# Where the running sums of a conditioning vector lie, and which engine adds to them

## The chip, the cores and the metric

The kernel runs on one core of one Trainium2 chip. The metric is the device time of one execution in microseconds (us), smaller is better. Three runs of the kernel before gave 2071.96, 2072.45 and 2074.96 us, so the median is 2072.45 us. A further execution was taken with the hardware profiler, and all rows of the profile come from that one.

## What is computed

One decoder layer, 1024 positions of width 2048, all in fp32. Cut to what matters here:

```python
mod = silu(c) @ W_ada + b_ada            # (1, 6144): shift | scale | gate, 2048 each
h   = rms_norm(x) * (1 + scale) + shift  # (1024, 2048)
proj = h @ W_in                          # (1024, 8192): q,k,v,z of 8 + 8 heads
...                                      # stick-breaking attention, retention, gating
out = x + gate * (concat(oa, ob) @ W_out)
```

`mod` is a product of one row of 2048 numbers with a matrix of 2048 x 6144, so W_ada is 48 MB that is read once and used for one multiply-add for each number. This is the *conditioning*. `h`'s first 1024 columns need only the first half of shift and scale. So the kernel computes the first half of the conditioning at its start, begins with the first half of the depth of `h @ W_in`, and does the conditioning's second half (the rest of shift and scale, and the gate) beside those matmuls. The change is in that second half.

## The kernel before, in words

**The large products.** Each of the three fp32 products is cut into groups of 256 output columns and half of the depth. A group is done with seven products instead of eight (a Strassen-Winograd scheme: `P1` to `P7`, line 32), each of depth 512 in four steps. An fp32 operand is split in a high and a low part, and a step is three matmuls 128x128 by 128x512 (`mm3`, lines 149 to 152), so a product is 12 matmuls. There are 16 groups in the first stage (`groups_a`); its tiles are named with an `e` in the profile: `b_e`, `a_e`, `d_e` are PSUM banks that take products, `wr_e` the raw weights, `wh_e_P` and `wl_e_P` their high and low parts. For every product ScalarE (ACT) makes the high part (line 259) and VectorE (DVE) the low part (line 264: raw minus high, both from SBUF); GpSimd (POOL) makes sums and differences of weight blocks (line 254); DVE also adds finished banks onto tiles in SBUF (line 293, one operand in PSUM) and ACT copies banks out (line 284). The third matmul of a step in the program's order uses `wl_e_P` (line 152 in the profile).

**The order of the work.** Each engine works through a list in order, and these lists are written out by the program itself, not by a scheduler: one *tick* is one step of a product (three matmuls). `at(k, fn)` records `fn`'s instructions k ticks later; generators such as `second_half` are continued when the number of ticks that they yielded has passed. So the place of every instruction in its engine's queue is fixed by ticks, and at run time an engine that waits holds up all that stands behind it. All the large loads and stores are issued from one queue (SyncE, SP), also in order.

**The second half of the conditioning** (`second_half`, lines 592 to 653). Line 408 views W_ada so that partition p holds rows 16p to 16p+15. For each of eight column blocks i of 512 columns, 16 tiles 128x512 (r = 0 to 15) are loaded into a ring of four buffers (`sg`, shown as `ada_b`), three rows ahead; the load of row n+3 takes the buffer of row n-1. Rows come every 2 or 3 ticks. Row r of block i is handled so:

- For i below 4 (shift and scale) DVE does all 16 rows with `weigh`: the first is a multiplication by the column `silu_c[:, r]` (line 433), the other 15 are `acc = row * column + acc` in one instruction (SCALAR_TENSOR_TENSOR, line 435). The running sum `acc_b` lies in SBUF.
- For i from 4 on (the gate) DVE does the even rows alone. Odd rows are multiplied by ACT (line 631 for r = 1, line 633 in place for the others) and added to a second running sum by POOL (line 635, two ticks later). The buffer of such a row is free when POOL has added it.

Ten ticks after a block's last row, `close` sums over the partitions (`over_partitions`, lines 410 to 414): the running sum is the matmuls' weight operand, four 128x128 pieces, and a column of ones is the moving operand. With two running sums there are eight such matmuls. The profile shows two records for each, so 8 records in a close for i below 4 and 16 for i from 4 on. The result is one column of a PSUM bank (`mod_b`, bank C), from which DVE takes it three ticks later (lines 419 to 421, or 617).

`keep_left` (lines 655 to 664) runs beside it: POOL adds high and low parts into `kp` tiles (line 661) and SP stores them. PSUM has eight banks: four for the products (`pj0` to `pj3`), and `A0`, `A1`, `B`, `C`. In the stretch of `second_half` the program uses of the latter four only `C`.

Of the kernel before, what the change touches and what calls it, by code (L numbers as in the profile page):

```python
# [11 lines left out]
F32 = mybir.dt.float32  # L12
F32R = mybir.dt.float32r
I32 = mybir.dt.int32
AF = mybir.ActivationFunctionType
ALU = mybir.AluOpType

P = 128
# [8 lines left out]
HALF = 512  # L27
# [32 lines left out]
def layer_kernel(ctx, tc, x, c, w_ada, b_ada, norm_gain, w_in, sb_q_gain, sb_k_gain, ret_norm_gain, w_out,  # L60
                 rot, ret_mask, ret_kdec, chunk_decay, out):
    nc = tc.nc
# [7 lines left out]
    ps = ctx.enter_context(tc.tile_pool(name="ps", bufs=1, space=PS))  # L70
# [36 lines left out]
    silu_c = cons.tile([P, 16], F32, name="silu_c")  # L107
# [57 lines left out]
    def at(k, fn):  # L165
        later.append((now[0] + k, fn))
# [243 lines left out]
    def over_partitions(mod, accs_):  # L410
        for i in range(4):
            for acc in accs_:
                nc.tensor.matmul(mod[:, i:i + 1], acc[:, i * P:(i + 1) * P], ones, start=acc is accs_[0],
                                 stop=acc is accs_[-1])

    def ada_mod(j, mod):

        k2 = slice(2 * j, 2 * j + 2)
        nc.vector.tensor_tensor(a_c[:, k2], mod[:, 2:4], scale_b1[:, k2], op=ALU.add)
        nc.vector.tensor_tensor(a_c[:, k2], a_c[:, k2], gain_c[:, k2], op=ALU.mult)  # L420
        nc.vector.tensor_tensor(s_c[:, k2], mod[:, 0:2], shift_b[:, k2], op=ALU.add)
# [4 lines left out]
    def to_h(t, kc):  # L426
        nc.scalar.activation(t, t, AF.Identity, scale=a_c[:, kc:kc + 1], bias=s_c[:, kc:kc + 1])

    def weigh(acc, src, r, first):

        cj = silu_c[:, r:r + 1]
        if first:
            nc.vector.tensor_scalar(acc, src, cj, None, op0=ALU.mult)
        else:
            nc.vector.scalar_tensor_tensor(acc, src, cj, acc, op0=ALU.mult, op1=ALU.add)  # L435
# [153 lines left out]
    k1b = Ring(k1p2.__enter__())  # L589
    ctx.enter_context(tc.manual_schedule(engines=set(ENGINES)))  # L590

    def second_half():

        order_ = [(i, r) for i in range(8) for r in range(16)]
        src, accs_ = {}, {}

        def load(n):
            if n < len(order_):
                i, r = order_[n]
                src[i, r] = t = k1b.tile([P, HALF], F32, tag="sg", bufs=4, name=f"ada_b{i}_{r}")  # L600
                if i < 4:
                    j = NP + i
                    nc.sync.dma_start(t.rearrange("p (a n) -> p a n", a=2),
                                      ada_rows[:, r, 0:2, 256 * j:256 * j + 256])
                else:
                    nc.sync.dma_start(t, ada_rows[:, r, 2, HALF * (i - 4):HALF * (i - 3)])

        def close(i):
            mod = ps.tile([P, 4], F32, tag="C", name=f"mod_b{i}")
            over_partitions(mod, accs_.pop(i))  # L610

            def take_mod():
                if i < 4:
                    ada_mod(NP + i, mod)
                else:
                    k4 = slice(4 * (i - 4), 4 * (i - 3))
                    nc.vector.tensor_tensor(gate_c[:, k4], mod, gate_b[:, k4], op=ALU.add)
            at(3, take_mod)

        for n in range(3):  # L620
            load(n)
        yield 9
        for n, (i, r) in enumerate(order_):
            if r == 0:
                accs_[i] = [k1b.tile([P, HALF], F32, tag="acc", bufs=2, name=f"acc_b{i}")]
            t = src.pop((i, r))
            if i < 4 or r % 2 == 0:
                weigh(accs_[i][0], t, r, r == 0)
            elif r == 1:
                accs_[i].append(k1b.tile([P, HALF], F32, tag="acc2", bufs=2, name=f"acc2_b{i}"))  # L630
                nc.scalar.activation(accs_[i][1], t, AF.Copy, scale=silu_c[:, r:r + 1])
            else:
                nc.scalar.activation(t, t, AF.Copy, scale=silu_c[:, r:r + 1])
                a2 = accs_[i][1]
                at(2, lambda a2=a2, t=t: nc.gpsimd.tensor_tensor(a2, a2, t, op=ALU.add))
            if r == 15:
                at(10, lambda i=i: close(i))
            load(n + 3)
            yield 2 + n % 2
        yield 16  # L640
        for j in range(NP):
            kc = KC // 2 + 2 * j
            a11, a12, a21, a22 = xT[kc, 0], xT[kc + 1, 0], xT[kc, 1], xT[kc + 1, 1]
            for t, k in ((a11, kc), (a21, kc), (a22, kc + 1), (a12, kc + 1)):
                to_h(t, k)
                yield 2
            s1 = k1b.tile([P, HALF], F32, tag="sg", bufs=4, name=f"S1_{j}")
            nc.gpsimd.tensor_tensor(s1, a21, a22, op=ALU.add)
            yield 2
            nc.gpsimd.tensor_tensor(a21, a11, a21, op=ALU.subtract)  # L650
            yield 2
            staged.update({("A11", j): a11, ("S3", j): a21, ("S1", j): s1, ("A12", j): a12, ("A22", j): a22})
        ready.add("h2")

    def keep_left():
# [8 lines left out]
        ready.add("keep")  # L664

    start(second_half(), 4)
    start(keep_left(), 40, 0)

# [693 lines left out]
```

## Time and profile before

| what | value |
|---|---|
| median of three runs | 2072.45 us |
| the profiled execution's own time | 2072.09 us |
| its span from first to last instruction | 2070.3 us |
| mean granted TensorE clock | 0.98 |
| PE busy | 1957.0 us, 95% of the span |
| DVE, ACT, POOL busy | 1427.0, 941.0, 925.6 us |
| first and last multiply-add of the second half | 132.6 and 377.8 us after the span's start |

Between the span and the execution's own time lie 1.8 us that no instruction shows. The conditioning's second half takes the stretch from about 130 to 385 us, about an eighth of the span.

How rows are read: a group of instructions is given as line, engine, operation, output <- inputs, shapes, count, then busy time in us and mean ns of one, and behind the second bar the idle time of the engine just before them and what ended it. In rows of three durations these are the shortest, the median and the longest, in ns. A row of waits gives the waiting engine with its tile and line, what it waited for, us in total, how often, and the longest. A row of a window gives from and to, its length, and for each engine busy us and the number of instructions, then the granted clock (`PEclk`), the busy share of the DMA engines, and GB/s.

### The profile page before, as it was taken

To read this page: it belongs to the slowest core of one execution; us is meant where nothing else is said; L and a number is where in the kernel's file an instruction comes from. 1 tells how busy PE (TensorE), PEld (TensorE's weight loads), DVE (VectorE), ACT (ScalarE), POOL (GpSimd) and SP (SyncE) were. 2 spreads that over 40 slices of the span, in tenths; PEclk is the share of its full clock that TensorE was granted. 3 is DMA by queue.
4 is the path that set the end of the run, shared out by engine and by line. 5 is a ranking of instruction groups with operands and counts; after the bars stand their busy time and mean duration, and the time that the engine had idled before them with its cause. 6 is when DMAs were issued, how large, how long until landed. Compare 5 with 4: busy or idle time off the path is not lost. (4 is left out here: it accounts for less than half of the span.)

```text
span 2070.3 us, 27207 instructions
## 1 busy us (share of the span) xinstructions
PE 1957.0 (95%) x9089; PEld 1564.0 (76%) x9089; DVE 1427.0 (69%) x2098; ACT 941.0 (45%) x1718; POOL 925.6 (45%) x627
## 2 busy tenths in 40 slices
PE   5879999998999999999999999899999998998998
PEld 4458777775768677788888888687788876886887
DVE  6779877566668675776766655788687887448555
ACT  4443344554455545554444444544353545345222
POOL 0434577765444235232322312677465654145443
PEclk9879999999999999999999999999999999999999
DMA  8748877533454444443433523867576877457665
GB/s 295 234 126 275 269 235 255 163 107 117 151 171 153 138 143 163 146 160 115 158 121 112 177 93 128 273 214 260 190 257 214 275 257 238 145 170 236 199 197 175
DMA packets 287329, 388.45 MB, mean 188 GB/s; under 512 B 32106, under 2 KB 164276, under 8 KB 287188
## 3 DMA queue, kind: packets, MB, share of 16 engines
q1 hardware_dynamic: 286784, 386.65, 56.9%
q8 instruction: 72, 1.18, 0.2%
q14 instruction: 69, 0.57, 0.1%
q10 hardware_dynamic: 404, 0.05, 0.0%
HBM read 278.51 MB, written 108.10 MB: 187 GB/s over the span
## 5 line engine op out<-in xcount | busy, mean ns | idle before, releaser
L264 DVE TENSOR_TENSOR wl_e_P<-wr_e,wh_e_P 128x512 fp32r<-128x512 f32 x560 | 528.9, 945 | 218.1 <-ACT wh_e_P L259 213.1
L254 POOL TENSOR_TENSOR wr_e<-wr_e,wr_e 128x512 f32<-128x512 f32 x240 | 354.6, 1492 | 495.3 <-DVE wl_e_P L264 445.7
L259 ACT ACTIVATE wh_e_P<-wr_e 128x512 fp32r<-128x512 f32 x560 | 350.7, 628 | 276.1 <-PE b_o L151 28.1
L254 POOL TENSOR_TENSOR wr_e<-wr_e 128x512 f32<-128x512 f32 x80 | 112.9, 1411 | 134.5 <-DVE wl_e_P L264 120.3
L915 DVE TENSOR_TENSOR_SCAN om<-om 128x128 f32<-128x128 f32 (+2 forms) x96 | 120.1, 1251 | 56.7 <-ACT om L906 54.9
L287 POOL TENSOR_TENSOR u_e<-u_e,c_e 128x512 f32<-128x512 f32 x50 | 79.0, 1583 | 114.9 <-DMA c_e<-part 71.8
L287 POOL TENSOR_TENSOR p_e<-p_e,c_e 128x512 f32<-128x512 f32 x49 | 74.9, 1529 | 102.2 <-DMA c_e<-part 59.4
L435 DVE SCALAR_TENSOR_TENSOR acc_b<-ada_b,silu_c,acc_b 128x512 f32<-128x512 f32 x88 | 97.3, 1106 | 27.4 <-DMA ada_b<-in_w_ada_dram 26.9
L152 PE MATMUL b_e<-S_h,wl_e_P 128*128 128x512 f32 x192 | 77.6, 404 | 7.9 <-DVE wl_e_P L264 7.7
L150 PE MATMUL b_e<-S_h,wh_e_P 128*128 128x512 f32 x192 | 77.1, 401 | 5.7 <-ACT p_e L284 5.7
L921 DVE TENSOR_TENSOR be<-be,om 128x127 f32<-128x127 f32 (+2 forms) x96 | 76.0, 792 | 7.8
L152 PE MATMUL b_h<-S_h,wl_e_P 128*128 128x512 f32 x192 | 75.7, 394 | 4.2 <-DVE wl_e_P L264 4.2
L151 PE MATMUL b_h<-S_l,wh_e_P 128*128 128x512 f32 x192 | 75.3, 392 | 3.4 <-DVE S_l L147 2.4
L962 PE MATMUL oT<-a,v 128*128 128x256 f32 x320 | 76.8, 379 | 0.0
L150 PE MATMUL b_h<-S_h,wh_e_P 128*128 128x512 f32 x192 | 76.7, 400 | 0.0
L151 PE MATMUL b_e<-S_l,wh_e_P 128*128 128x512 f32 x192 | 76.5, 398 | 0.0
L150 PE MATMUL b_f<-S_h,wh_e_P 128*128 128x512 f32 x192 | 76.3, 398 | 0.0
L150 PE MATMUL b_g<-S_h,wh_e_P 128*128 128x512 f32 x192 | 75.8, 395 | 0.0
L152 PE MATMUL b_f<-S_h,wl_e_P 128*128 128x512 f32 x192 | 74.9, 390 | 0.4 <-DVE wl_e_P L264 0.4
L151 PE MATMUL b_f<-S_l,wh_e_P 128*128 128x512 f32 x192 | 74.9, 390 | 0.0
L152 PE MATMUL b_g<-S_h,wl_e_P 128*128 128x512 f32 x192 | 74.9, 390 | 0.0
L151 PE MATMUL b_g<-S_l,wh_e_P 128*128 128x512 f32 x192 | 74.9, 390 | 0.0
(487 smaller groups left out, 5505.8 us busy)
## 6 DMA issues: line engine op xcount, KB each, us to landing
wr_e<-in_w_in_dram SPq DMA_DIRECT2D x128, 512.0 KB, 5.5
ada_b<-in_w_ada_dram SPq DMA_DIRECT2D x128, 256.0 KB, 4.7
c_e<-part SPq DMA_DIRECT2D x128, 256.0 KB, 5.2
ada_a<-in_w_ada_dram SPq DMA_DIRECT2D x64, 256.0 KB, 4.4
wr_e<-in_w_out_dram SPq DMA_DIRECT2D x32, 512.0 KB, 4.8
ld<-fin SPq DMA_DIRECT2D x54, 256.0 KB, 4.7
part<-p_e SPq DMA_DIRECT2D x48, 256.0 KB, 5.3
part<-u_e SPq DMA_DIRECT2D x48, 256.0 KB, 2.1
```

The lines of the kernel that those rows point to most:

```text
L150: nc.tensor.matmul(o, a_hi, b_hi, start=first, stop=False, skip_group_check=True)
L151: nc.tensor.matmul(o, a_hi, b_lo, start=False, stop=False, skip_group_check=True)
L152: nc.tensor.matmul(o, a_lo, b_hi, start=False, stop=last, skip_group_check=True)
L254: nc.gpsimd.tensor_tensor(t[o], t[a], t[b], op=op)
L259: nc.scalar.activation(hi, self.t[RIGHT[p]], AF.Copy)
L264: nc.vector.tensor_tensor(lo, self.t[RIGHT[p]], self.parts[p].bitcast(F32), op=ALU.subtract)
L287: at(6, lambda: nc.gpsimd.tensor_tensor(t, t, o, op=ALU.add))
L435: nc.vector.scalar_tensor_tensor(acc, src, cj, acc, op0=ALU.mult, op1=ALU.add)
L915: nc.vector.tensor_tensor_scan(rev, rev, rev, init, op0=ALU.mult, op1=ALU.bypass)
L921: nc.vector.tensor_tensor(be[:, :m], be[:, :m], om[:, 1:m + 1], op=ALU.mult)
L962: nc.tensor.matmul(ob, v[:, j, :], a[:, cl], start=diag and ib == 0 and b == 0 and j2 == 0, stop=ch == 0 and ib == 2, skip_group_check=True)
```

## The change

The running sum `acc` of each of the eight blocks becomes a PSUM tile of 128x512, one whole bank, `A0` for even i and `A1` for odd i. DVE does all 16 rows of every block, for the gate too; ACT's multiplications and POOL's additions of odd rows (lines 631, 633, 635) and the second running sum are gone. Two ticks after a block's last row ACT copies the bank once into an SBUF tile `total` (`acc_s`), and `close`, at the same tick as before, sums that one tile over the partitions. Loads, their order, their buffers and the ticks are as they were.

```diff
             if r == 0:
-                accs_[i] = [k1b.tile([P, HALF], F32, tag="acc", bufs=2, name=f"acc_b{i}")]
-            t = src.pop((i, r))
-            if i < 4 or r % 2 == 0:
-                weigh(accs_[i][0], t, r, r == 0)
-            elif r == 1:
-                accs_[i].append(k1b.tile([P, HALF], F32, tag="acc2", bufs=2, name=f"acc2_b{i}"))
-                nc.scalar.activation(accs_[i][1], t, AF.Copy, scale=silu_c[:, r:r + 1])
-            else:
-                nc.scalar.activation(t, t, AF.Copy, scale=silu_c[:, r:r + 1])
-                a2 = accs_[i][1]
-                at(2, lambda a2=a2, t=t: nc.gpsimd.tensor_tensor(a2, a2, t, op=ALU.add))
+                acc = ps.tile([P, HALF], F32, tag=f"A{i % 2}", name=f"acc_b{i}")
+            weigh(acc, src.pop((i, r)), r, r == 0)
             if r == 15:
-                at(10, lambda i=i: close(i))
+                total = k1b.tile([P, HALF], F32, tag="acc", bufs=2, name=f"acc_s{i}")
+                at(2, lambda total=total, acc=acc: nc.scalar.activation(total, acc, AF.Copy))
+                at(10, lambda i=i, total=total: close(i, total))
```

`close` then calls `over_partitions(mod, [acc])` with that one tile.

How the queues change, first on DVE at the start of block i = 6 (`gate_c` closes block 5; `wl_e_P` is the low part of a weight, `u_e` and `p_e` take a finished bank). Before:

```order
L433 TENSOR_SCALAR acc_b_1317<-ada_b_0_1270,silu_c 128x512
L264 TENSOR_TENSOR wl_e_P_1263<-wr_e_0_1192,wh_e_P_1255 128x512
L435 SCALAR_TENSOR_TENSOR acc_b_1317<-ada_b_2_1274,silu_c,acc_b_1317 128x512
L264 TENSOR_TENSOR wl_e_P_1194<-wr_e_1_1199,wh_e_P_1190 128x512
L264 TENSOR_TENSOR wl_e_P_1201<-wr_e_0_1192,wh_e_P_1197 128x512
L617 TENSOR_TENSOR gate_c<-mod_b_2659,cols 128x4
```

The same place on DVE now:

```order
L433 TENSOR_SCALAR acc_b_2617<-ada_b_0_1270,silu_c 128x512
L264 TENSOR_TENSOR wl_e_P_1263<-wr_e_0_1192,wh_e_P_1255 128x512
L435 SCALAR_TENSOR_TENSOR acc_b_2617<-ada_b_1_1272,silu_c,acc_b_2617 128x512
L435 SCALAR_TENSOR_TENSOR acc_b_2617<-ada_b_2_1274,silu_c,acc_b_2617 128x512
L264 TENSOR_TENSOR wl_e_P_1194<-wr_e_1_1199,wh_e_P_1190 128x512
L435 SCALAR_TENSOR_TENSOR acc_b_2617<-ada_b_3_1319,silu_c,acc_b_2617 128x512
L264 TENSOR_TENSOR wl_e_P_1201<-wr_e_0_1192,wh_e_P_1197 128x512
L617 TENSOR_TENSOR gate_c<-mod_b_2652,cols 128x4
```

Each odd row of a gate block now stands on DVE between the low parts, 32 such instructions in all, as it did before for blocks 0 to 3.

On ACT, at the end of block 5 (`acc_s` is `total`, `wh_e_P` the high part of a weight, `p_e` and `c_e` copies of finished banks), now:

```order
L284 ACTIVATE p_e_1373<-b_e_2570 128x512
L259 ACTIVATE wh_e_P_1197<-wr_e_0_1192 128x512
L629 ACTIVATE acc_s_1730<-acc_b_2400 128x512
L259 ACTIVATE wh_e_P_1255<-wr_e_0_1192 128x512
L284 ACTIVATE c_e_1715<-b_e_2419 128x512
```

The copy out of PSUM (line 629 of the changed kernel) is new; it stands ahead of the next high part, and it must wait for DVE's last row of that block.

On PE, the close of block 5, before (the two tiles are DVE's and POOL's running sums):

```order
L152 MATMUL b_e_2577<-S_3_h,wl_e_P_1201 128x512
L413 MATMUL mod_b_2659<-ones,acc_b_1525 128x1
L413 MATMUL mod_b_2659<-ones,acc_b_2408 128x1
L413 MATMUL mod_b_2659<-ones,acc_b_1525 128x1
L413 MATMUL mod_b_2659<-ones,acc_b_2408 128x1
L413 MATMUL mod_b_2659<-ones,acc_b_1525 128x1
L413 MATMUL mod_b_2659<-ones,acc_b_2408 128x1
L413 MATMUL mod_b_2659<-ones,acc_b_1525 128x1
L413 MATMUL mod_b_2659<-ones,acc_b_2408 128x1
L150 MATMUL d_e_2672<-S_0_h,wh_e_P_1255 128x512
```

and now:

```order
L151 MATMUL b_e_2570<-S_3_l,wh_e_P_1197 128x512
L152 MATMUL b_e_2570<-S_3_h,wl_e_P_1201 128x512
L413 MATMUL mod_b_2652<-ones,acc_s_1730 128x1 x4
L150 MATMUL d_e_2661<-S_0_h,wh_e_P_1255 128x512
L151 MATMUL d_e_2661<-S_0_l,wh_e_P_1255 128x512
```

Four of the eight matmuls of each gate block's close are gone; for blocks 0 to 3 the count stays at four.

More of the change, by code (lines that the diff above doesn't have):

```diff
@@ L594, in second_half @@
         order_ = [(i, r) for i in range(8) for r in range(16)]
-        src, accs_ = {}, {}
+        src = {}
         def load(n):
@@ L606, in load, with close @@
                     nc.sync.dma_start(t, ada_rows[:, r, 2, HALF * (i - 4):HALF * (i - 3)])
-        def close(i):
+        def close(i, acc):
             mod = ps.tile([P, 4], F32, tag="C", name=f"mod_b{i}")
-            over_partitions(mod, accs_.pop(i))
+            over_partitions(mod, [acc])
             def take_mod():
```

## The prediction, made before the changed kernel ran

> **What bounds the kernel now.** The page first, for who is busy; then the groups of DVE in the stretch of the second half; then windows between the closes, for where PE loses time; then waits and single durations, for why.
>
> ```profile
> PE 1957.0 (95%) x9089; PEld 1564.0 (76%) x9089; DVE 1427.0 (69%) x2098; ACT 941.0 (45%) x1718; POOL 925.6 (45%) x627
> core 0: us, PE busy (x) PEld busy (x) DVE busy (x) ACT busy (x) POOL busy (x), PEclk, DMA share, GB/s
> 163.00:193.00 30.00, 29.90 (x139) 24.54 (x139) 26.50 (x32) 10.47 (x18) 15.15 (x11) 1.00 0.89 289
> 193.00:223.00 30.00, 28.05 (x119) 21.73 (x118) 27.29 (x35) 8.22 (x14) 13.77 (x9) 1.00 0.72 236
> 223.00:255.00 32.00, 29.33 (x131) 23.41 (x131) 25.81 (x33) 8.62 (x15) 15.08 (x10) 1.00 0.85 276
> 286.00:317.00 31.00, 29.71 (x132) 23.46 (x132) 23.04 (x22) 13.42 (x23) 24.69 (x16) 1.00 0.73 243
> 317.00:351.00 34.00, 31.95 (x130) 24.57 (x130) 25.63 (x23) 14.60 (x26) 25.21 (x18) 0.90 0.83 282
> ```
>
> PE is the bound: the time is PE's work plus the gaps in it. In this stretch DVE is busy for 74 to 91% of a window, and PE has gaps.
>
> How much is lost shows between the closes. From the timeline of PE, the closes of blocks 0, 4 and 7:
>
> ```profile
> 161.68 0.39 PE L152 MATMUL b_e<-S_h,wl_e_P 128*128 128x512 f32 x1
> 163.04 0.39 PE L152 MATMUL b_e<-S_h,wl_e_P 128*128 128x512 f32 x1
> 163.27 0.95 PE L413 MATMUL mod_b<-ones,acc_b 128*128 128x1 f32 x8
> 164.40 0.39 PE L151 MATMUL b_e<-S_l,wh_e_P 128*128 128x512 f32 x1
> ...
> 284.97 0.39 PE L152 MATMUL b_e<-A_h,wl_e_P 128*128 128x512 f32 x1
> 285.20 1.92 PE L413 MATMUL mod_b<-ones,acc_b 128*128 128x1 f32 x16
> 287.29 0.40 PE L151 MATMUL d_e<-A_l,wh_e_P 128*128 128x512 f32 x1
> ...
> 383.16 2.15 PE L413 MATMUL mod_b<-ones,acc_b 128*128 128x1 f32 x16
> ```
>
> Six matmuls from 161.68 to 163.04 give a pitch of 0.227 us, so a product of 12 takes 2.72. A close of 8 records puts 164.40 - 163.04 = 1.36 where two pitches (0.45) would stand: it costs 0.91. One of 16 costs 2.32 - 0.45 = 1.87. Between two closes lie 40 ticks, 120 matmuls, 27.2 us. From 163.27 to 383.16 are 219.9 us; seven times 27.2 is 190.4, and the seven closes in it (four short, three long) 9.25. So 20.2 us are lost, 2.9 for each block. Who is waited for:
>
> ```profile
> PE b_e L152 <- DVE wl_e_P L264: 3.1, 6, 0.8
> PE d_e L152 <- DVE wl_e_P L264: 1.9, 2, 1.3
> ...
> SPq L606 <- POOL acc_b L635: 51.8, 19, 6.0
> SPq L606 <- DVE acc_b L435: 12.3, 12, 3.1
> ...
> 319.40 0.49 DVE L433 TENSOR_SCALAR acc_b<-ada_b,silu_c 128x512 f32<-128x512 f32 x1 [4.47 <-DMA ada_b<-in_w_ada_dram]
> ...
> 319.00:320.00 1.00, 0.89 (x2) 0.16 (x2) 0.60 (x2) 0.00 (x0) 0.00 (x0) 0.51 1.06 394
> 325.00:326.00 1.00, 1.00 (x4) 0.81 (x3) 0.24 (x1) 0.87 (x3) 1.00 (x2) 0.58 1.05 391
> ```
>
> These waits are of 252 to 390 us. PE waits for the low parts, thus for DVE. SP's queue stood 51.8 us waiting for POOL to free row buffers, loads came late, and DVE waited for rows with low parts queued behind (4.47 us before 319.40, for the first row of block 6). There PE's granted clock fell to a half from 319 to 325.6: 3.3 of the 20.2 us are clock, 16.9 waits.
>
> **The change part by part.** Why DVE is late, for 125 to 252 us (blocks 0 to 3), then for 252 to 390:
>
> ```profile
> L435 DVE SCALAR_TENSOR_TENSOR acc_b<-ada_b,silu_c,acc_b 128x512 f32<-128x512 f32 x60 | 61.1, 1019 | 11.4 <-DMA ada_b<-in_w_ada_dram 10.8
> L264 DVE TENSOR_TENSOR wl_e_P<-wr_e,wh_e_P 128x512 fp32r<-128x512 f32 x41 | 36.2, 883 | 8.1 <-ACT wh_e_P L259 8.1
> ...
> L264 DVE TENSOR_TENSOR wl_e_P<-wr_e,wh_e_P 128x512 fp32r<-128x512 f32 x44 | 58.7, 1335 | 10.8 <-ACT wh_e_P L259 10.8
> L435 DVE SCALAR_TENSOR_TENSOR acc_b<-ada_b,silu_c,acc_b 128x512 f32<-128x512 f32 x28 | 36.2, 1293 | 16.1 <-DMA ada_b<-in_w_ada_dram 16.0
> L433 DVE TENSOR_SCALAR acc_b<-ada_b,silu_c 128x512 f32<-128x512 f32 x4 | 3.4, 856 | 5.4 <-DMA ada_b<-in_w_ada_dram 5.4
> L635 POOL TENSOR_TENSOR acc_b<-acc_b,ada_b 128x512 f32<-128x512 f32 x28 | 43.8, 1564 | 15.6 <-ACT ada_b L633 15.1
> ```
>
> And single durations (shortest, median, longest), of instructions with two inputs in SBUF and with one in PSUM:
>
> ```profile
> L435 DVE SCALAR_TENSOR_TENSOR acc_b<-ada_b,silu_c,acc_b x88: 735/753/1787, 132.6 to 377.8; 128x512 f32<-128x512 f32 x88
> L264 DVE TENSOR_TENSOR wl_e_P<-wr_e,wh_e_P x560: 617/691/1819, 95.6 to 2055.4; 128x512 fp32r<-128x512 f32 x187
> L293 DVE TENSOR_TENSOR c_e<-b_h,c_e x16: 673/682/692, 1341.6 to 1715.1; 128x512 f32<-128x512 f32 x16
> L295 DVE SCALAR_TENSOR_TENSOR cp_o<-b_o,gate_c,cp_o x7: 749/751/752, 1940.0 to 2062.8; 128x512 f32<-128x512 f32 x7
> L284 ACT ACTIVATE c_e<-b_e x16: 577/598/600, 144.4 to 469.4; 128x512 f32<-128x512 f32 x16
> ```
>
> Where both inputs lie in SBUF, DVE takes 0.69 to 0.75 us or up to 1.82; with one in PSUM never over 0.752. Low parts take 883 ns on average beside a POOL without running sums and 1335 beside one with them. I read the long ones as DVE and POOL shutting each other out of SBUF.
>
> *Multiply-adds.* The 88 become 120. With the sum in PSUM the nearest row is L295's 0.75, the same operation with one input in PSUM; but it writes SBUF, and no row has DVE write PSUM. Bounds: 0.735, the shortest in SBUF, and two passes, 1.47. I take 0.75. First rows (0.48 in SBUF at best, 0.86 in the gate) I put at no more than 0.75 too.
>
> *Low parts.* With 28 POOL additions gone, the gate blocks look like blocks 0 to 3: 883 for 1335. Bounds 617 and 1335.
>
> *DVE's need for one product.* Ten products carry 16 rows. Before, blocks 0 to 3: rows 1.6 x 1.0 = 1.6, the low part 0.88, additions of banks (three of seven products) 3/7 x 0.68 = 0.29: 2.8, and with 11.7 us of waits for rows (10.8 in the row above, and 0.9 for first rows in the row below) over 41 products 0.3 more: 3.1. PE needs 2.72 + 0.09 (a close) = 2.81. The gate: 0.7 x 1.29 + 0.1 x 0.86 + 1.34 + 0.29 = 2.6, and 21.4 us over 44 products 0.5: 3.1. Both halves are over PE's pace, and 219.9 / 70 = 3.14 us is the pace measured. After: 1.6 x 0.75 + 0.88 + 0.29 = 2.37; with waits for rows of 0.3 it is 2.65, under 2.81, with 0.5 it is 2.86, just over.
>
> ```profile
> DVE acc_b L433 <- DMA ada_b<-in_w_ada_dram: 0.9, 1, 0.9
> ```
>
> *What stays lost.* The row nearest to 2.37 of 2.81 (84%) is the window 163 to 193, where DVE was 88% busy. It ended with the close of block 1 at 191.89:
>
> ```profile
> 191.89 0.95 PE L413 MATMUL mod_b<-ones,acc_b 128*128 128x1 f32 x8
> ```
>
> 28.62 - 27.2 - 0.91 = 0.5 us lost. At 0.5 a block 3.5 us stay; at today's 2.9 all 20.2. I take 1.0 a block, above the near row because all blocks now carry 16 rows on DVE and rows can still come late: 7. So 13.2 us go, the 3.3 of the clock among them.
>
> *The clock.* The fall began right behind PE's long close of block 5:
>
> ```profile
> 317.25 1.72 PE L413 MATMUL mod_b<-ones,acc_b 128*128 128x1 f32 x14 [0.19 <-POOL acc_b L635]
> ```
>
> The only gap there was 0.19 us, a wait for POOL's running sum, which the change takes out, and the close is halved; so I count the fall as gone, though one event shows no rule. The Trainium skill ("TensorE: Matmul & The Clock Gate", Part 1) has the half clock follow an idle window of about 3.4 us. This trace disagrees: the clock fell with no such window. By that rule nothing here called for the fall, nothing in the change need remove it, and the sum would be 3.3 higher, 2058.4.
>
> *Closes.* Four go from 1.87 to 0.91: 3.8 us of PE's own work, off the path for certain.
>
> *Taken off, hidden.* ACT loses 32 multiplications, POOL 43.8 us; neither bounds PE. SP's loads then wait for DVE alone, as in blocks 0 to 3. The cover there is DVE's being on time; without it rows come late as today.
>
> *Added waits.* Eight copies out of PSUM, 0.6 us each by L284, on ACT with half its time free. Each waits for DVE's row 15, with the high part of a weight queued behind it, and low part and PE behind that. High parts are made two products (5.4 us) ahead, so a DVE late by under about 2 us costs nothing; beyond that it could cost up to 2 us eight times. It lies within the 7 that stay. The close has eight ticks (5.4 us) after the copy.
>
> **Sum.** 2072.1 (the profiled execution; the three runs' median is 0.4 above it) - 13.2 - 3.8 = 2055.1. With nothing lost it is 2072.1 - 24.0 = 2048.
>
> **The rivals.**
>
> *Rows still come late (2066).* DMA share is 0.72 to 0.89 over these windows, and 1.05 in single ones. The same bytes in 28.1 instead of 31.4 us raise 0.8 to 0.9. If it is the transfers, not the buffers, that make rows late, the 16.9 us of waits stay, only closes and perhaps the clock are won: 2065 to 2068. For it: DVE waited 11.7 us for rows also in blocks 0 to 3, where POOL holds no buffer. There SP waited so:
>
> ```profile
> SPq L603 <- DVE acc_b L435: 50.7, 45, 3.0
> ```
>
> Against: those are 45 short waits, the ring of four doing its work, and each late one had DVE late; in the gate it was 19 long ones. 0.17.
>
> *PSUM cannot be read and written at this rate in one instruction (slower).* DVE then needs 0.88 + 0.29 + 1.6 p for a product. At p = 1.47 that is 3.52, and 80 products at 3.52 for 3.14 are 30 us: 2102. With waits for rows of 0.3 it decides from p = 1.04 on. For it: no row shows the form. Against: reading a bank costs DVE nothing over SBUF (0.751 against 0.753). 0.08.
>
> *Given back at the end of the stage (2072).* When the first stage hands over to the second, PE is idle for 4.9 and 7.0 us while new left operands are made:
>
> ```profile
> 450.00:475.00 25.00, 20.07 (x78) 14.89 (x77) 23.87 (x21) 14.55 (x28) 19.13 (x13) 0.93 0.34 107
> 475.00:500.00 25.00, 18.01 (x62) 11.29 (x61) 18.13 (x16) 11.73 (x22) 14.80 (x10) 0.86 0.31 100
> ```
>
> If something there ends at a time that PE does not set, such as the stores of `kp`, an earlier PE waits longer. Against: all of it is recorded by PE's ticks and moves with them. 0.09.
>
> **How the numbers follow.** My forecast has 0.66, reaching from 2048 to 2061 (loss from nothing to 1.9 a block). 2055 is its middle sum. The range adds the first rival, to 2068; the slow case and the given-back case stay outside. A measurement of this kernel can tell about 0.2%, 4.1 us, from no change. Faster by more: the forecast, and 0.12 of the first rival: 0.78. Within: 0.05 of it and the given-back case, less a little: 0.13. Slower: 0.09.
>
> **What would show it.** Right: multiply-adds at 0.74 to 0.76 with the longest below 0.8; low parts from 250 to 380 us near 0.9; closes with 8 records; about 28 us from close to close; SP waiting for DVE alone. Wrong: multiply-adds over 1.05 us; DVE's waits for rows still over 30 us in total; closes 31 us apart; PE idle in the handover for 10 us more than before; or a stalled high part behind the copy.

## The result, and the profile after

The changed kernel is faster, by more than was forecast: four runs give 2046.24 to 2048.50 us, median 2047.38, beside 2071.96 to 2075.61, median 2073.70, for four runs of the kernel before. The ratio is 0.9866, with a 95% interval of 0.985 to 0.9882. The forecast was 2055 with a range from 2048 to 2068; the median lies 0.6 us below it. The profiled execution has a span of 2046.7 us where the one before had 2070.3. So this pair differs by 23.6 us (the 17.0 of the forecast stand beside that), and the medians by 26.3. The four runs of the kernel before lie within 3.7 us, and 22 more, taken beside the experiments, range from 2068.50 to 2080.03; a miss of 0.6 us is small beside that.

PE's timeline at the closes of blocks 0 and 7, then windows cut from close to close (from and to, length, then busy us of PE, weight loads, DVE, ACT and POOL; granted clock, DMA share, GB/s):

```profile
162.99 0.95 PE L413 MATMUL mod_b<-ones,acc_s 128*128 128x1 f32 x8
...
359.69 0.95 PE L413 MATMUL mod_b<-ones,acc_s 128*128 128x1 f32 x8
```

```profile
219.19:247.29 28.10, 28.10 (x129) 23.42 (x128) 23.68 (x33) 9.69 (x17) 12.85 (x10) 1.00 0.94 323
247.29:275.39 28.10, 28.10 (x129) 23.43 (x128) 25.44 (x36) 9.23 (x16) 12.81 (x10) 1.00 0.85 271
...
331.59:359.69 28.10, 28.10 (x130) 23.42 (x128) 20.44 (x30) 9.21 (x16) 12.21 (x9) 1.00 0.84 274
sum 196.70, PE 196.70 PEld 163.94 DVE 160.35 ACT 67.27 POOL 91.21; mean PE 28.10 PEld 23.42 DVE 22.91 ACT 9.61 POOL 13.03
```

All seven blocks take 28.10 us, to the hundredth: 27.2 of products and one short close of 0.91. PE is busy for 196.70 of 196.70 us: no gap is left. The last close comes 23.5 us earlier than before (383.16), the first only 0.3. From first to last close 219.89 - 196.70 = 23.2 us are gone: the 20.2 that were lost, and three closes shorter by about 0.95 each. The fourth long close is the last one itself, and its saving comes behind 383.16, so that PE is 24.7 us ahead from there on (the first use of a product's low part, at 399.3 us before, is at 374.6 now). Of these, 1.1 us are lost again after 1350 us, where both kernels have the same program; that may be a part of the 2.7 us between the two differences, and no row shows the rest.

Single durations (shortest, median, longest) on DVE and ACT; then the groups of low parts for 125 to 252 us and for 252 to 390:

```profile
L435 DVE SCALAR_TENSOR_TENSOR acc_b<-ada_b,silu_c,acc_b x120: 740/749/758, 132.3 to 353.1; 128x512 f32<-128x512 f32 x120
L433 DVE TENSOR_SCALAR acc_b<-ada_b,silu_c x8: 742/746/754, 129.6 to 327.4; 128x512 f32<-128x512 f32 x8
L629 ACT ACTIVATE acc_s<-acc_b x8: 595/597/602, 158.2 to 354.9; 128x512 f32<-128x512 f32 x8
```

```profile
L264 DVE TENSOR_TENSOR wl_e_P<-wr_e,wh_e_P 128x512 fp32r<-128x512 f32 x44 | 40.9, 929 | 11.5 <-ACT wh_e_P L259 11.4
...
L264 DVE TENSOR_TENSOR wl_e_P<-wr_e,wh_e_P 128x512 fp32r<-128x512 f32 x50 | 44.7, 895 | 21.9 <-ACT wh_e_P L259 21.8
```

The multiply-add into PSUM takes 749 ns, and 758 at the longest, where into SBUF it took up to 1787. The low parts, still with both inputs in SBUF, stay as they were in blocks 0 to 3 (929 beside 883) and fall from 1335 to 895 in the gate. Who waited, for the load queue and for DVE, in the same two stretches; from 125 to 390 us this view has no row for PE at all:

```profile
SPq L603 <- DVE acc_b L435: 36.8, 42, 2.5
DVE acc_b L435 <- DMA ada_b<-in_w_ada_dram: 8.1, 9, 2.0
...
SPq L606 <- DVE acc_b L435: 30.6, 36, 2.2
DVE acc_b L435 <- DMA ada_b<-in_w_ada_dram: 8.9, 8, 2.1
DVE acc_b L433 <- DMA ada_b<-in_w_ada_dram: 1.2, 1, 1.2
```

DVE's waits for rows fall from 33.1 us (11.7 and 21.4) to 18.2, and POOL is gone from the load queue's waits for row buffers. The handover to the second stage is as it was, some 25 us earlier: PE idle for 4.9 and 7.1 us.

```profile
425.00:450.00 25.00, 20.09 (x78) 14.95 (x77) 23.59 (x21) 14.40 (x27) 19.11 (x14) 0.93 0.33 101
450.00:475.00 25.00, 17.92 (x62) 11.28 (x61) 18.45 (x17) 12.00 (x22) 14.55 (x10) 0.86 0.33 104
```

### The profile page after: what moved, and what is told of

The parts are those of the page before. It is cut to its first block, busy times and chain, and to the rows that moved or that the text cites. A ratio compares the mean times of both kernels' runs of the same rounds, so it can differ in the third digit from the quotient of the medians.

```text
span 2046.7 us, 27175 instructions
## 1 busy us (share of the span) xinstructions
PE 1943.6 (95%) x9057; PEld 1560.4 (76%) x9057; DVE 1406.4 (69%) x2130; ACT 925.8 (45%) x1694; POOL 864.4 (42%) x599
## 5 line engine op out<-in xcount | busy, mean ns | idle before, releaser
L264 DVE TENSOR_TENSOR wl_e_P<-wr_e,wh_e_P 128x512 fp32r<-128x512 f32 x560 | 515.6, 921 | 226.3 <-ACT wh_e_P L259 221.4
L254 POOL TENSOR_TENSOR wr_e<-wr_e,wr_e 128x512 f32<-128x512 f32 x240 | 345.6, 1454 | 517.1 <-DVE wl_e_P L264 463.0
L435 DVE SCALAR_TENSOR_TENSOR acc_b<-ada_b,silu_c,acc_b 128x512 f32<-128x512 f32 x120 | 90.0, 750 | 18.0 <-DMA ada_b<-in_w_ada_dram 17.0
```

Source lines behind the costliest of these rows:

```text
L254: nc.gpsimd.tensor_tensor(t[o], t[a], t[b], op=op)
L264: nc.vector.tensor_tensor(lo, self.t[RIGHT[p]], self.parts[p].bitcast(F32), op=ALU.subtract)
```

## Experiments

Two questions were open. Which part of the change took the stalls away, and why nothing at all was lost, with DVE 82% busy (160.35 of 196.70 us), where the forecast left 1.0 us a block. Each ratio below is to the kernel before, with its 95% interval; besides, I use the length from first to last close (219.89 us before, 196.70 after), which the trace gives to the hundredth.

**All rows on DVE, sums in SBUF.** The change's other half alone: in the kernel before, the odd rows of the gate go to DVE too.

```diff
-            if i < 4 or r % 2 == 0:
-                weigh(accs_[i][0], t, r, r == 0)
-            elif r == 1:
...
+            weigh(accs_[i][0], src.pop((i, r)), r, r == 0)
```

> All 16 rows of every block on VectorE as in the changed kernel, but the running sums stay in SBUF, with no copy out; closes have 8 records. Theory (VectorE overloaded by being shut out of SBUF): one product needs 1.6 rows x about 1.0 us + 0.88 + 0.29 + 0.05 = 2.8 us, and with the waits for rows about 3.1, over TensorE's 2.81 as blocks 0 to 3 of the kernel before; the blocks are about 31 us apart after the first two, 219.9 us of the kernel before from first to last close become about 215, and the span is about 2066 us. Rival (GpSimd's additions of odd rows, which held row buffers and the load queue, were the whole cause): the gate's blocks lose nothing, only blocks 1 to 3 the 7 us that they lost before; about 204 us from first to last close, span about 2054 us.

Measured: 2066.3 us median, ratio 0.9958 (0.994 to 0.9976), span 2066.4, 213.83 us from first to last close. Blocks 0 to 1, 1 to 2, 3 to 4 and the sum, then the multiply-adds for 125 to 252 us and, with the low parts, for 252 to 390:

```profile
162.79:191.43 28.64, 28.52 (x130) 23.26 (x128) 25.45 (x32) 9.84 (x17) 14.13 (x10) 1.00 0.88 293
191.43:222.59 31.16, 29.42 (x129) 23.03 (x128) 28.61 (x36) 8.88 (x16) 14.74 (x10) 1.00 0.72 235
...
253.24:284.58 31.34, 29.62 (x129) 23.03 (x128) 29.42 (x33) 8.86 (x15) 16.49 (x11) 1.00 0.77 251
...
sum 213.83, PE 203.22 PEld 162.07 DVE 190.97 ACT 64.68 POOL 103.39; mean PE 29.03 PEld 23.15 DVE 27.28 ACT 9.24 POOL 14.77
```

```profile
L435 DVE SCALAR_TENSOR_TENSOR acc_b<-ada_b,silu_c,acc_b 128x512 f32<-128x512 f32 x60 | 61.7, 1029 | 10.8 <-DMA ada_b<-in_w_ada_dram 10.2
...
L435 DVE SCALAR_TENSOR_TENSOR acc_b<-ada_b,silu_c,acc_b 128x512 f32<-128x512 f32 x60 | 63.9, 1064 | 10.5 <-DMA ada_b<-in_w_ada_dram 10.0
L264 DVE TENSOR_TENSOR wl_e_P<-wr_e,wh_e_P 128x512 fp32r<-128x512 f32 x47 | 43.9, 936 | 6.6 <-ACT wh_e_P L259 6.6
```

As the theory had it: POOL's additions are gone, and still every block but the first loses 2 to 4 us. Against the changed kernel only the place of the sum differs (and eight copies): 1029 and 1064 ns for 749, and 213.83 - 196.70 = 17.1 us. So with all rows on DVE the place of the sum is worth 17.1 of the 23.2 us.

**Sums in PSUM, work split as before.** DVE's sums lie in PSUM and are copied out by ACT; ACT and POOL keep the odd rows of the gate.

```diff
-                accs_[i] = [k1b.tile([P, HALF], F32, tag="acc", bufs=2, name=f"acc_b{i}")]
+                accs_[i] = [ps.tile([P, HALF], F32, tag=f"A{i % 2}", name=f"acc_b{i}")]
...
+                def copy_out(i=i):
+                    total = k1b.tile([P, HALF], F32, tag="acc", bufs=2, name=f"acc_s{i}")
+                    nc.scalar.activation(total, accs_[i][0], AF.Copy)
+                    accs_[i][0] = total
+                at(2, copy_out)
```

> The running sums that VectorE makes lie in PSUM and are copied out by ScalarE, but odd rows of the gate's blocks stay with ScalarE and GpSimd as in the kernel before; closes of the gate have 16 records again. Theory: blocks 0 to 3 lose nothing; in the gate one product needs 0.8 x 0.75 + 1.34 + 0.29 + 0.05 = 2.3 us, with waits for rows of up to 0.5 just about TensorE's 2.8, so at most 3 us are lost there; with 3.8 us of longer closes the span is 2050 to 2054 us. Rival (GpSimd's additions holding row buffers and the load queue): the gate still loses its 9.6 us of waits and perhaps the 3.3 us of the clock, span 2060 to 2064 us.

Measured: 2059.93 us, ratio 0.9923 (0.9902 to 0.9943), span 2058.4. Blocks 3 to 4, 5 to 6 and 6 to 7, then what ended waits in 252 to 390 us:

```profile
248.28:276.38 28.10, 28.10 (x130) 23.42 (x129) 19.82 (x26) 13.56 (x24) 22.41 (x16) 1.00 0.75 240
...
305.37:340.04 34.67, 32.12 (x137) 25.06 (x136) 19.44 (x24) 15.04 (x27) 23.70 (x18) 0.95 0.81 277
340.04:372.24 32.20, 30.80 (x137) 25.52 (x136) 22.23 (x26) 14.68 (x25) 25.20 (x18) 0.95 0.77 253
```

```profile
SPq L606 <- POOL acc_b L635: 49.5, 21, 6.1
DVE acc_b L435 <- DMA ada_b<-in_w_ada_dram: 22.6, 10, 4.3
DVE acc_b L433 <- DMA ada_b<-in_w_ada_dram: 6.7, 2, 6.3
```

Up to the close of block 4 all blocks take 28.10 us: for blocks 0 to 3 PSUM alone does it. In the gate my theory falls. With its long closes a block should take 29.0 (shown below); the last two take 34.67 and 32.20, so 8.9 us are lost there though DVE is busy for only 56 and 69% of them. DVE waited 29 us for rows, and the load queue 49.5 us for POOL. That is the rival's cause. Its size is smaller: the rival had 9.6 us of waits and perhaps 3.3 of the clock, and of the 8.9 some 3.4 are the clock (shown below); the span lies under its 2060 to 2064. With the work split, the place of DVE's sums is worth 11.6 us from first to last close (219.89 less 208.26, from 163.98 to 372.24).

**The same split, with rows set free early.** ACT writes its product into another tile, not over the row.

```diff
-                nc.scalar.activation(t, t, AF.Copy, scale=silu_c[:, r:r + 1])
-                a2 = accs_[i][1]
+                s = k1b.tile([P, HALF], F32, tag="acc", bufs=2, name=f"scaled_{i}_{r}")
+                nc.scalar.activation(s, t, AF.Copy, scale=silu_c[:, r:r + 1])
+                t, a2 = s, accs_[i][1]
```

> The split kernel with VectorE's sums in PSUM (odd rows of the gate by ScalarE and GpSimd), but ScalarE writes its product to a tile of its own instead of over the row, so that the row's buffer is free when ScalarE is done and does not wait for GpSimd's addition. Theory (what the gate lost in the split kernel, 8.7 us between closes 5 and 7, came from row buffers held by GpSimd, thus late loads): the load queue no longer waits for GpSimd, VectorE's waits for rows fall from 29 to under 15 us in the gate, and its blocks are 29.1 us apart; span about 2051 us. Rival (VectorE shut out by GpSimd's additions in its low parts): the gate still loses about 8 us, span about 2058 us.

Measured: 2050.35 us, ratio 0.9881 (0.9863 to 0.99), span 2047.6, 3 us under the theory's. The last block, then waits and groups of DVE and POOL in 252 to 390 us:

```profile
332.45:361.45 29.00, 29.00 (x138) 24.32 (x137) 18.22 (x23) 12.89 (x22) 23.93 (x18) 1.00 0.81 268
```

```profile
DVE acc_b L435 <- DMA ada_b<-in_w_ada_dram: 9.6, 7, 2.1
...
L264 DVE TENSOR_TENSOR wl_e_P<-wr_e,wh_e_P 128x512 fp32r<-128x512 f32 x49 | 52.1, 1063 | 35.8 <-ACT wh_e_P L259 33.3 <-PE d_e L152 2.4
L435 DVE SCALAR_TENSOR_TENSOR acc_b<-ada_b,silu_c,acc_b 128x512 f32<-128x512 f32 x26 | 19.4, 747 | 9.6 <-DMA ada_b<-in_w_ada_dram 9.6
...
L636 POOL TENSOR_TENSOR acc_b<-acc_b,acc_s 128x512 f32<-128x512 f32 x27 | 38.9, 1441 | 15.3 <-ACT acc_s L634 14.9
```

PE has no gap, there or in any block of the gate, and the load queue's list of waits has no row for these additions. So the gate's loss in the split kernel was the row buffers that POOL held, not POOL's work. From first to last close this kernel takes 199.38 us (from 162.07), 2.7 more than the changed one, which is its three long closes: with the sums in PSUM and the rows set free early, giving the odd rows to DVE gains the shorter closes and nothing else. The rows show the other effect side by side too: beside 27 more additions on POOL the low parts take 1063 ns, the multiply-adds into PSUM 747. The Trainium skill ("SBUF — State Buffer", Who interferes with whom) says that a DVE instruction with two SBUF inputs contends with a GpSimd instruction that reads SBUF, and that one with at most one such input does not, outside the modes in which it uses two ports; these rows agree.

**Long closes alone.** The changed kernel, its gate closes joined by four matmuls with a tile of zeros.

```diff
-            over_partitions(mod, [acc])
+            over_partitions(mod, [acc, zero] if i >= 4 else [acc])
...
+        zero = k1b.tile([P, HALF], F32, tag="zero", bufs=1, name="acc_zero")
+        nc.vector.memset(zero, 0.0)
```

> The changed kernel with closes of 16 records again in the gate's four blocks: the four matmuls with the sum are joined by four with a tile of zeros. Theory (the closes are TensorE's own work, 0.96 us more each, and nothing else): the blocks after the gate's closes are 29.1 us apart instead of 28.1, last close 2.9 us later, span about 2050.5 us, granted clock 1.00 all through the stretch. Rival (the long closes, not the waits, made the clock fall to a half): the clock falls behind at least one of them and 3.3 us more are lost.

Measured: 2051.25 us, ratio 0.989 (0.9866 to 0.9913), span 2048.8. The blocks 3 to 4 and 6 to 7:

```profile
248.72:276.82 28.10, 28.10 (x129) 23.42 (x128) 24.35 (x36) 9.24 (x16) 12.70 (x10) 1.00 0.85 277
...
334.81:363.81 29.00, 29.00 (x138) 24.31 (x137) 22.10 (x31) 9.21 (x16) 11.88 (x10) 1.00 0.83 269
```

0.9 us a close and no more, and the clock stays at 1.00 through the gate. In the split kernel it fell to a half twice, from 309.9 to 313.3 and from 344.0 to 347.4 us; 6.8 us at a half cost 3.4. The first fall came 2 us behind a long close, when PE had just waited 1.51 us for a low part, the second behind a long close in which it had waited 1.41 us for POOL's sum:

```profile
309.39 0.50 PE L152 MATMUL d_e<-S_h,wl_e_P 128*128 128x512 f32 x1 [1.51 <-DVE wl_e_P L264]
...
311.00:312.00 1.00, 1.00 (x4) 0.50 1.05 399
...
341.73 0.38 PE L413 MATMUL mod_b<-ones,acc_b 128*128 128x1 f32 x2 [1.41 <-POOL acc_b L635]
...
344.00:345.00 1.00, 1.00 (x5) 0.51 0.89 326
```

So long closes without a wait did not make the clock fall (four here, and four in the split kernel with rows set free early). With the fall in the kernel before there are three in this stretch, each beside a long close with a wait in it or just behind it. But the kernel with sums in SBUF, whose closes are short, kept 1.00 through waits of up to 1.4 us, and in the handover of the changed kernel the clock fell at 440.9 us behind a wait of 1.98 us with no close near. What makes it fall stays open.

**How much DVE can take.** The changed kernel with one needless multiplication of a row into a spare bank for every fourth, second, or each row (`r % 4 == 1`, `r % 2 == 1`, or no condition).

```diff
-            weigh(acc, src.pop((i, r)), r, r == 0)
+            t = src.pop((i, r))
+            if r % 4 == 1:
+                more = ps.tile([P, HALF], F32, tag="B", name=f"more_{i}_{r}")
+                nc.vector.tensor_scalar(more, t, silu_c[:, r:r + 1], None, op0=ALU.mult)
+            weigh(acc, t, r, r == 0)
```

> The changed kernel with one needless multiplication of a row into a spare PSUM bank (0.75 us on VectorE) for every fourth row, 32 in all. VectorE's need for a product goes from 2.46 to 2.76 us, of TensorE's 2.81 (98%). Theory (a threshold: nothing is lost while the need is under TensorE's pace, as the queue runs two products ahead): under 2 us lost, span 2047 to 2049 us. Rival (loss grows smoothly with VectorE's load, the idea behind the 7 us in the forecast): at least the 2.9 us a block of the kernel before, span about 2067 us.

> As before, but a needless multiplication for every second row, 64 in all. The need is 3.06 us for a product, 0.25 over TensorE's 2.81. Theory (threshold with a reserve of two products, 5.4 us): 80 products x 0.25 - 5.4 = 14.6 us lost, none in the first block or two and then 2.5 us a block, span about 2061 us, and VectorE's waits for rows nearly gone since rows are there before it gets to them. Rival (smooth loss, and waits for rows that stay at 18 us): 80 x 0.48 = 38 us less the reserve, span 2080 us, loss in every block.

> The changed kernel with a needless multiplication for every row, 128 in all. Theory 1 (VectorE's need is the sum of the durations in the rows): 2.46 + 1.6 x 0.75 = 3.66 us a product, 0.85 over TensorE's 2.81, 80 x 0.85 - 5.4 = 63 us lost, span about 2110 us. Theory 2 (instructions of VectorE that follow each other start about 0.08 us before the end in the row of the one before, so a product needs 0.08 less for each of its three to five instructions): 2.21 + 1.6 x 0.67 = 3.28 us, 0.47 over, 80 x 0.47 - 5.4 = 32 us lost, span about 2079 us, blocks near 32.8 us apart. In both VectorE's waits for rows all but vanish.

Measured: every fourth, 2048.91 us, ratio 0.9874 (0.9851 to 0.9897), span 2047.7; every second, 2055.44, ratio 0.9901 (0.9879 to 0.9923), span 2053.6; each, 2069.54, ratio 0.9981 (0.9971 to 0.999), span 2066.7. The sums over the seven blocks, in this order:

```profile
sum 198.60, PE 197.85 PEld 163.63 DVE 171.53 ACT 67.66 POOL 91.65; mean PE 28.26 PEld 23.38 DVE 24.50 ACT 9.67 POOL 13.09
```

```profile
sum 202.72, PE 199.66 PEld 162.89 DVE 185.52 ACT 67.49 POOL 90.84; mean PE 28.52 PEld 23.27 DVE 26.50 ACT 9.64 POOL 12.98
```

```profile
sum 218.84, PE 206.54 PEld 161.37 DVE 216.29 ACT 67.75 POOL 88.30; mean PE 29.51 PEld 23.05 DVE 30.90 ACT 9.68 POOL 12.61
```

The first part of each is the length: 196.70, 198.60, 202.72, 218.84 with 0, 32, 64 and 128 needless instructions, so 1.9, 6.0 and 22.1 us lost. The loss is not proportional: a quarter of the load costs a twelfth, the last half costs three quarters. The theory held for every fourth row (under 2 us). For every second row it was too high, 6.0 us where it had 14.6, and the rival's 33 (38 less the reserve) is further off. At 128 DVE is busy for 216.29 of 218.84 us; it is the bound there, at 3.13 us a product.

For each row both theories put the need too high (63 and 32 us lost). The timeline of DVE in that kernel shows why the first did:

```profile
300.56 0.74 DVE L628 TENSOR_SCALAR more<-ada_b,silu_c 128x512 f32<-128x512 f32 x1
301.22 0.74 DVE L435 SCALAR_TENSOR_TENSOR acc_b<-ada_b,silu_c,acc_b 128x512 f32<-128x512 f32 x1
301.87 0.74 DVE L628 TENSOR_SCALAR more<-ada_b,silu_c 128x512 f32<-128x512 f32 x1
```

An instruction of 0.74 us is followed after 0.65 to 0.66. The low parts were shorter as well: their mean was 738 and 792 ns in the two stretches, where I had taken 0.9. With both, 2 x 1.6 x 0.66 + (0.765 - 0.08) + 3/7 x 0.61 + 0.05 (taking a close) = 3.11, near the pace measured. The waits for rows did not vanish with 64 (17.1 us stayed, the rival's 18), only with 128 (1.8 us). With these waits, divided by 80 products, all three come out, though this sum was made after the runs: the need by starts and the waits are about 2.45 + 0.26 = 2.7 us a product with 32 (measured 2.84, PE's own 2.81), 2.67 + 0.21 = 2.9 with 64 (2.90), and 3.1 with 128 (3.13). With 32 the mean is still under PE's pace; 1.4 of the 1.9 us went in one block, in which DVE waited for two late rows in short order (2.15 us before 224.50 and 1.68 before 228.53). So the loss begins a little before the mean need reaches the pace. ACT's copies waited longer too (16.0 us in eight waits with 64, 3.8 the longest), with high parts queued behind them; what that cost was not measured by itself.

## Why the prediction was wrong

The mechanism was right and so was the sign; the size was off by one term, the loss that was to stay. The traces show how far DVE runs ahead of PE: a product's low part is ready at one time, and the first matmul that uses it starts later. The lead is the time from the end of the first row of a pair (its start plus its length) to the start of the second. Two products in the kernel before, then the second of them in the changed kernel:

```profile
160.08 0.68 DVE L264 TENSOR_TENSOR wl_e_P<-wr_e,wh_e_P 128x512 fp32r<-128x512 f32 x1
164.62 0.39 PE L152 MATMUL b_e<-S_h,wl_e_P 128*128 128x512 f32 x1
...
185.61 0.68 DVE L264 TENSOR_TENSOR wl_e_P<-wr_e,wh_e_P 128x512 fp32r<-128x512 f32 x1
186.38 0.45 PE L152 MATMUL d_e<-S_h,wl_e_P 128*128 128x512 f32 x1
```

```profile
182.67 0.68 DVE L264 TENSOR_TENSOR wl_e_P<-wr_e,wh_e_P 128x512 fp32r<-128x512 f32 x1
186.10 0.39 PE L152 MATMUL d_e<-S_h,wl_e_P 128*128 128x512 f32 x1
```

Before, the lead falls from 3.86 to 0.09 us inside the window from 163 to 193. In the changed kernel the second product still has 2.75, and from first to last close the lead never falls below 1.1 us.

- **What stays lost: wrong, the step that failed.** The forecast left 7 us, 1.0 a block, and nothing was lost. The 0.5 us of the window 163 to 193 were read as what a DVE at 88% costs PE. But that window was no steady state: DVE was falling behind there, and its lead over PE was being used up (the rows above); the next two blocks lost 3.3 and 3.6 us (31.40 and 31.69 from close to close). The kernel with sums in SBUF does the same (28.64, then 31.16). In the changed kernel a block with DVE 91% busy (25.44 of 28.10 us) loses nothing, because the lead covers it. The forecast's own sum, 2.37 and 0.3 of waits under 2.81, already said zero, and a row from a kernel whose need was over PE's pace was put above it. That DVE's need was a little overstated, by 0.08 us an instruction, points the same way.
- **Multiply-adds: right.** 0.75 us taken, 749 ns measured; the first rows 746 (at most 0.75 was taken).
- **Low parts: right in the gate** (883 taken, 895 measured). The reason given was POOL's running sums. With these gone and DVE's sums still in SBUF the mean fell from 1335 to 936 ns; with these kept and DVE's sums in PSUM it was 1063. So they are the larger part, and the place of DVE's own sums counts as well.
- **Why rows came late: right, but under-used.** The page of waits showed SP standing 51.8 us for POOL. The forecast took it for one cause among others; the two split kernels show that in the gate it alone kept PE waiting once the sums lay in PSUM (8.9 us, some 3.4 of them by the clock, and 0 without it).
- **Closes: right within 0.3.** 3.8 us taken; 0.9 us each by the long-close kernel, 3.6 for four.
- **Clock: right that the fall goes.** What makes it fall was only argued: a long close alone did not.
- **Added waits: right.** ACT waited three times, 4.0 us in all, for a bank to copy, and PE for none of it.
- **The rivals.** Late rows by transfers did not come: the DMA share rose to 0.84 to 0.94, and waits for rows fell. The slow form in PSUM did not come: 758 ns at the longest. The gain was not given back there: the handover lost 11.9 us before and 12.0 after.

The range ended at 2048, where all of the loss in the profiled execution is gone. That left nothing for the 2.7 us by which medians and profiles differ, nor for the scatter of the runs; had the median come 0.6 us later, inside the range, this step would have failed all the same.

## What to carry to other kernels

Look for a queue's need against the pace of what it feeds, start to start and waits included, not for its busy share: while it is under the pace the loss can be zero, as here with DVE 82% busy, and a window in which a lead is being used up shows neither the loss before it nor the one after. Where DVE and POOL both work on SBUF, an accumulator that DVE alone adds to can lie in a free PSUM bank, so that each row costs one SBUF input (749 ns for 1029 here). And a ring of buffers is as slow as its slowest holder: ask which engine gives a buffer back, and what stands behind the load that waits for it.

## What the runs showed of the hardware

- A SCALAR_TENSOR_TENSOR on DVE that reads and writes its running sum in one PSUM bank (128x512 fp32, the other input in SBUF) takes 740 to 758 ns, about as long as the undisturbed form in SBUF (735 at the shortest, 753 the median), and it does not lengthen beside a busy POOL: the mean was 747 where POOL was busy for 23.93 of 29.00 us.
- TENSOR_SCALAR from SBUF takes 742 to 754 ns into PSUM, where into SBUF it took 475 at the shortest.
- Rows of DVE overlap: one of 0.74 us is followed after 0.65 to 0.66.
- TensorE's granted clock fell to a half, for 3.4 us twice and for nearly 7 once, beside closes of 16 records (eight one-column matmuls) with a wait in them (0.19 and 1.41 us) or 2 us behind them (1.51 us), and not behind eight such closes without a wait.
